# A hybrid decoder layer on one core: the bonus products of the recurrence move behind the projections that cover the inverse

## The chip, the core and the metric

The kernel runs on one core of a Trainium2 chip. The engines of that core are TensorE (PE, matmuls; PEld is its weight load), VectorE (DVE), ScalarE (ACT), GpSimd (POOL) and SyncE (SP, which here issues the DMAs). Every engine has its own queue and works it off in order; engines wait for each other through semaphores. The metric is the device time of one execution in microseconds; less is better.

## The reference

One layer for 512 prompt tokens and 8 x 8 sample tokens (576 columns in all), with 1024 channels. A normed input is projected by one large matrix `w_in`, whose columns feed three branches and their gates; the branches are merged and projected again. Only the first branch, an RWKV-7 recurrence with 16 heads of 64, is touched by the change:

```python
def step(s, inp):
    r_t, k_t, v_t, w_t, kk_t, a_t = inp
    sa = jnp.einsum("bhvk,bhk->bhv", s, -kk_t)
    s = (s * w_t[:, :, None, :] + sa[..., None] * (kk_t * a_t)[:, :, None, :]
         + v_t[..., None] * k_t[:, :, None, :])
    return s, jnp.einsum("bhvk,bhk->bhv", s, r_t)
...
bonus = jnp.sum(r * k * r_k.astype(f32), axis=-1, keepdims=True) * v
out = (o + bonus.reshape(bsz, t, RW_WIDTH)) * jax.nn.silu(z.astype(f32))
```

The `bonus` is a sum over the 64 channels of a head, times `v`. It is added to the recurrence's output only at the end; nothing in the recurrence needs it.

## The kernel before

**The stream of projections.** All projections by `w_in` are cut into units of 128 output channels (class `Unit`). The class `Stream` runs them in steps: one step is 6 matmuls of 128x288 (three products of high and low parts, two halves of the columns), and 8 steps make a unit. `st.go(n)` (L381) runs n steps, so PE has work while another engine prepares the next piece of the recurrence. There are two lists: units added with `st.add` go first, the others (gates `g`, `xb`, `zc`, `zb`) are fill, taken when the first list is empty. When a unit begins, the next one is picked and its weights are loaded (`weight`, L286): a DMA of 512 KB into `wraw`, a cast on ACT into `whi` (L293), and a subtraction on DVE into `wlo` (L294). `wraw`, `whi` and `wlo` have two buffers each, so the cast for a unit waits until PE has ended the unit before the one that begins.

**The recurrence.** `rwkv_phase` handles the 16 heads as 8 pairs, in four groups (0 to 3) of two pairs. The time axis is cut into chunks of 64. For each group, in the order of the code:
- `prep_a`, `prep_b`, `scaled`, `products`, `prep_c`: decay, keys and products of a chunk, the matrix `M1` among them.
- `substitute` (L1079): the inverse of the 32x32 triangular blocks, a chain of 30 pairs on DVE, a product into `Xt` (L1085) and an addition into `X` (L1087), each needing the one before. Then `X` is transposed into `XT` (L1091), and X and XT go by DMA to DRAM (`d2`, `d3`; both print as `d`) and back, into `M1` (L1101) and `xz` (L1098).
- `direct` (L1134): products R and Zt that need no inverse.
- `bonus` (L1011): for each pair of heads, `bonh` and `bonl` (high and low part of r k r_k), four matmuls with a block of ones into `bon`, and two products with `v` on DVE (L1020).
- `st.go(34)`: 34 steps of projections, the cover for the chain and its DMAs.
- `invert2` (L1104): products `z` and `w` of 32x32 that complete the inverse; `z` needs `xz`. It holds four steps of its own. `solved` (L1160): U and W.
- `lora_w(g + 1)` loads small weights of the next group, and `st.add(*group_units(g + 1))` puts its six projections (`u`, for k, r and v of two pairs) on the first list.
- `chain` (L1201), eight times: the chunks one after the other, with 2 and 4 steps of projections in each (1 and 3 in the last group). On DVE, `plus_state` (L1199) adds the state's part to UV, which the matmul `dS` then reads.
- Then `pairs(g + 1)` runs the stream until the next group's units are done, and `prep_a` of that group begins.

A framework orders the instructions of each engine by its own model of their times, unless `K.pin` is set: then PE keeps the order of the code. In the code before, it is set from `invert2` to the end of the chain. The output of a unit is taken by its `use`; that of a `u` unit needs copies on ACT and two operations on DVE (L923, L924).

Of the kernel before, what the change touches and what calls it, by code (L numbers as in the profile page):

```python
# [860 lines left out]
def rwkv_phase(K):  # L861
    nc, tc, i, pv, st = K.nc, K.tc, K.i, K.pv, K.st
    G = 2
    NG = KC // G
    H2 = 2 * NCH
    NQ = 2 * G * H2
    with ExitStack() as es:
# [65 lines left out]
        def group_units(g):  # L933
            out = []
            for tag, base in (("k", 8), ("r", 0), ("v", 16)):
                for p in range(G * g, G * g + G):
                    out.append(u_unit(base + p, tag))
            return out
# [46 lines left out]
        def prep_b(o):  # L985
            p, q = o.p, o.q
            br = o.br
            zs = 1 - q
            pr_ = K.psb("rs")
            for c in range(NCH):  # L990
                K.mm(pr_[br:br + 64, 2 * c:2 * c + 2], o.sq[:, C * c:C * c + C], K.bones2, start=True, stop=True,
                                 tile_position=(0, br))
            rvf = rsv[q][br:br + 64].rearrange("p c h -> p (c h)")
            nc.vector.tensor_scalar(rvf, pr_[br:br + 64, 0:18], -2.0, -2.0 * L2_EPS, op0=ALU.mult, op1=ALU.add)
            nc.vector.reciprocal(rvf, rvf)
            BK = o.BK = rg.tile([P, NCH, 2, C], F32, tag="BK", name="BK")
            ZR = o.ZR = rg.tile([P, NCH, 2, C], F32, tag="ZR", name="ZR")
            zn, ta, sq = o.zn, o.ta, o.sq
            nc.vector.tensor_mul(ZR[:, 0:8, zs, :], chk(zn)[:, 0:8, :], o.Pp[:, :, 0:C])
            nc.vector.tensor_mul(ZR[:, 8, zs, :].rearrange("p (b s) -> p b s", s=NS), smp(zn), o.Ps[:, :, 0:NS])  # L1000
            nc.vector.tensor_mul(ZR[:, 0:8, q, :], chk(o.r)[:, 0:8, :], o.Pp[:, :, 1:])
            nc.vector.tensor_mul(ZR[:, 8, q, :].rearrange("p (b s) -> p b s", s=NS), smp(o.r), o.Ps[:, :, 1:])
            nc.vector.scalar_tensor_tensor(sq, ta, 1.0, zn, op0=ALU.add, op1=ALU.mult)
            nc.vector.tensor_mul(BK[:, :, zs, :], chk(sq), chk(o.pinv))
            nc.scalar.activation(ta, ta, AF.Identity, scale=K.kah[:, p:p + 1], bias=K.kac[:, p:p + 1])
            nc.vector.tensor_mul(o.k, o.k, ta)
            nc.vector.tensor_mul(BK[:, :, q, :], chk(o.k), chk(o.pinv))
            nc.vector.tensor_mul(ta, o.r, o.k)
            o.bon = rg.tile([P, N], F32, tag="bon", name="bon")
# [12 lines left out]
        def scaled(o):  # L1022
            BK = o.BK
            BKn = o.BKn = rg.tile([P, NCH, P], F32, tag="BKn", name="BKn")
            for c in range(8):
                nc.scalar.activation(BKn[:, c, :], BK[:, c].rearrange("p w t -> p (w t)"), AF.Copy, scale=o.Pp[:, c, C:C + 1])
            nc.vector.tensor_mul(BKn[:, 8, :].rearrange("p (w b s) -> p w b s", w=2, s=NS),
                                 BK[:, 8].rearrange("p w (b s) -> p w b s", s=NS),
                                 o.Ps[:, :, NS:NS + 1].unsqueeze(1).to_broadcast([P, 2, NB, NS]))

        def products(o):

            q, BK, ZR = o.q, o.BK, o.ZR
            rv = rsv[q]
            M1 = o.M1 = rg.tile([P, H2, P], F32, tag="M1", name="M1")
            for c0, n in ((0, 4), (4, 4), (8, 1)):
                pms = [K.psb("m1") for h in range(2)]
                for c in range(c0, c0 + n):
                    for w in range(2):
                        for h in range(2):  # L1040
                            K.mm(pms[h][64 * w:64 * w + 64, P * (c - c0):P * (c - c0) + P],
                                             BK[64 * h:64 * h + 64, c, w, :],
                                             ZR[64 * h:64 * h + 64, c].rearrange("p a b -> p (a b)"), start=True, stop=True,
                                             tile_position=(64 * h, 64 * w))
                for h in range(2):
                    for c in range(c0, c0 + n):
                        nc.vector.scalar_tensor_tensor(M1[:, 2 * c + h, :], pms[h][:, P * (c - c0):P * (c - c0) + P],
                                                       rv[:, c, h:h + 1], maskq[q][c == 8],
                                                       op0=ALU.mult, op1=ALU.mult)
            for blk in range(2):  # L1050
                q0 = (blk * G + q) * H2
                a = o.br + 32 * blk
                nc.sync.dma_start(d1[0][q0:q0 + H2].rearrange("q s t -> s q t"), o.M1[a:a + 32, :, a:a + 32])
# [80 lines left out]
        def direct(prs):  # L1134

            r0 = prs[0].r0 = [rt.tile([P, N], F32, tag="k", name="r0") for _ in range(2)]
            for c0, n in ((0, 4), (4, 4), (8, 1)):
                pR = K.psb("R")
                for c in range(c0, c0 + n):
                    for h in range(2):  # L1140
                        for o in prs:
                            a, b, m = o.kr, o.br, P * (c - c0) + C * h
                            K.mm(pR[b:b + 64, m:m + C], o.M1[a:a + 64, 2 * c + h, b:b + 64],
                                             o.UV[a:a + 64, c, C * h:C * h + C], start=True, stop=True, tile_position=(a, b))
                if n == 4:
                    nc.scalar.copy(r0[c0 // 4][:, 0:P * n], pR)
                else:
                    for h in range(2):
                        nc.scalar.copy(r0[h][:, P * 4:N], pR[:, C * h:C * h + C])
            zt = prs[0].zt = [rt.tile([P, N], F32, tag="r", name="zt") for _ in range(2)]  # L1150
            for c0 in (1, 5):
                pZ = K.psb("Zt")
                for c in range(c0, c0 + 4):
                    for o in prs:
                        b, m = o.br, P * (c - c0)
                        K.mm(pZ[b:b + 64, m:m + P], o.ZR[:, c, 1 - o.q, :], K.ident, start=True, stop=True,
                                         tile_position=(0, b))
                nc.scalar.copy(zt[c0 // 4][:, 0:P * 4], pZ)
# [209 lines left out]
        for g in range(NG):  # L1368
            UV2[0] = rg.tile([P, G, NCH, P], F32, tag="UV", name="UV", bufs=1)
            d1[0] = dr.tile([NQ, 32, 32], F32, tag="d1", name="d1")  # L1370
            for o in prs:
                prep_b(o)
                st.go(3)
                scaled(o)
                products(o)
                st.go(3)
            X = invert()
            for o in prs:
                prep_c(o)
                st.go(3)  # L1380
            substitute(prs, X)
            direct(prs)
            for o in prs:
                bonus(o)
            st.go(34)
            K.pin = True
            invert2(prs)
            solved(prs)
            if g + 1 < NG:
                lora_w(g + 1)  # L1390
                st.add(*group_units(g + 1))
            o0, o1 = prs
            none = lambda: None
            fulls = {1: lambda: sample_a(o0), 4: lambda: sample_c(o0), 5: lambda: sample_a(o1)}
            tileds = {2: lambda: sample_b(o0), 3: lambda: [sample_o(o0), sample_in(o1)],
                      6: lambda: sample_b(o1), 7: lambda: sample_o(o1)}
            sample_in(o0)
            for c in range(8):
                chain(prs, c, (2, 4) if g + 1 < NG else (1, 3), fulls.get(c, none), tileds.get(c, none))
            K.pin = False  # L1400
            sample_c(o1)
            st.add(*[za_unit(o.p) for o in prs])
            nxt = pairs(g + 1) if g + 1 < NG else []
            for o in prs:
                state_out(o)
            gn_a()
            for o in nxt:
                prep_a(o)
                st.go(2)
            gn_t(prs)  # L1410
            for o in prs:
                gn_b(o)
            prs = nxt
# [70 lines left out]
def hybrid_step(ctx: ExitStack, tc: tile.TileContext, ins, outs):  # L1484
# [20 lines left out]
    with ExitStack() as es:  # L1505
# [34 lines left out]
        attention(K, pool(es, "xs"), qs, qf, kv)  # L1540
    K.softplus()
    rwkv_phase(K)
    st.until("zc7")
    o2 = pool(ctx, "o2")
# [66 lines left out]
```

## Time and profile before

| | us |
|---|---|
| median of 3 runs | 1204.92 |
| lowest and highest | 1202.93, 1207.01 |
| profiled execution | 1204.39 |
| its span | 1202.4 |
| PE busy | 1128.5 (94%) |
| DVE busy | 707.8 (59%) |
| ACT busy | 522.4 (43%) |

The mean granted clock of TensorE is 0.969 of full speed. A row of a timeline has the start, the duration, engine, line, operation, output<-input, shapes, count, and in brackets the idle time just before it with what ended it. A row of the waits has the total, the times and the longest. A row of the stretches has the length and then for PE, PEld, DVE, ACT and POOL the busy time and the count, then the granted clock, the busy share of the DMA engines and GB/s. All names of tiles are without buffer numbers.

### The profile page before, as it was taken

Reading aid. Unit: us, or ns where it says so; the run is one execution under the profiler, and the core shown is the slowest. Engines: PE = TensorE matmul, PEld = TensorE weight load, DVE = VectorE, ACT = ScalarE, POOL = GpSimd, SP = SyncE. Lnnn points to the kernel's source line nnn. Section 1 sums busy time; section 2 is a strip of 40 time slices with the busy share of each in tenths; the row PEclk is TensorE's granted clock in tenths of the full one; section 3 lists DMA queues with packets and bytes.
Section 4 is the critical chain, followed back from the end, with each engine's and each line's share of the span. In section 5 each row is a group of like instructions: output and inputs, shape, how many; then the busy total and the mean of one; then the engine's idle time right before and its main releaser. Section 6 shows DMA issues by size and latency. Waiting matters only on the chain.

```text
span 1202.4 us, 25686 instructions
## 1 busy us (share of the span) xinstructions
PE 1128.5 (94%) x10567; PEld 1066.5 (89%) x10567; DVE 707.8 (59%) x1454; ACT 522.4 (43%) x1004; POOL 152.7 (13%) x287
## 2 busy tenths in 40 slices
PE   5999999999979999969999789999799999999997
PEld 4998988899979998969998789989799999999997
DVE  5345655246773478734687724787456669684633
ACT  5444544246413374313464233653233576622333
POOL 3010000010001311002210003110032002020022
PEclk9999999999998998979999979999799999999999
DMA  4456756632242222332223423233434857466412
GB/s 138 127 193 194 227 176 226 201 94 80 76 142 75 68 65 88 107 94 82 67 81 93 131 64 89 64 88 100 128 105 139 284 151 219 130 218 188 123 46 79
DMA packets 220622, 151.49 MB, mean 126 GB/s; under 512 B 52640, under 2 KB 196106, under 8 KB 220506
## 3 DMA queue, kind: packets, MB, share of 16 engines
q1 hardware_dynamic: 217242, 146.87, 41.7%
q10 hardware_dynamic: 3264, 2.99, 0.9%
q8 instruction: 83, 1.36, 0.5%
q14 instruction: 33, 0.27, 0.1%
HBM read 120.82 MB, written 29.01 MB: 125 GB/s over the span
## 4 chain that ended last, share of the span: by engine, by line
PE 70%; DVE 14%; DMA 8%; ACT 4%; issue 3%; SPq 1%; ACTq 0%; DVEq 0%
PE u L71 14%; PE br L71 11%; PE g L71 7%; PE za L71 4%; PE fo L71 4%; PE q L71 4%; DVE wlo L294 3%; DVE X L1087 3%; DVE Xt L1085 3%; PE zc L71 2%; PE A L71 2%; PE zb L71 2%; PE xb L71 2%; PE kv L71 2%; DMA wraw<-in_w_mem_kv 1%
## 5 line engine op out<-in xcount | busy, mean ns | idle before, releaser
L293 ACT CAST whi<-wraw 128x1024 fp32r<-128x1024 f32 x129 | 135.2, 1048 | 284.8 <-issue 57.5
L294 DVE TENSOR_TENSOR wlo<-wraw,whi 128x1024 fp32r<-128x1024 f32 x128 | 156.7, 1224 | 168.3 <-ACT whi L293 167.0
L71 PE MATMUL u<-xh,whi 128*128 128x288 f32 x400 | 89.5, 305 | 0.0
L71 PE MATMUL g<-xh,whi 128*128 128x288 f32 x384 | 88.9, 312 | 0.0
L71 PE MATMUL g<-xh,wlo 128*128 128x288 f32 x384 | 87.4, 307 | 1.1 <-DVE wlo L294 1.1
L71 PE MATMUL g<-xl,whi 128*128 128x288 f32 x384 | 86.4, 306 | 0.0
L71 PE MATMUL u<-xl,whi 128*128 128x288 f32 x400 | 85.9, 296 | 0.0
L71 PE MATMUL u<-xh,wlo 128*128 128x288 f32 x400 | 85.8, 296 | 0.0
L71 PE MATMUL br<-oh,wlo 128*128 128x288 f32 x384 | 82.5, 297 | 1.4 <-DVE wlo L294 1.4
L71 PE MATMUL br<-oh,whi 128*128 128x288 f32 x384 | 83.5, 299 | 0.0
L71 PE MATMUL br<-ol,whi 128*128 128x288 f32 x384 | 82.2, 296 | 0.0
L71 PEld LDWEIGHTS u<-xh,whi 128*128 128x128 f32 x400 | 63.7, 189 | 6.5 <-issue 6.1
L71 PEld LDWEIGHTS g<-xh,wlo 128*128 128x128 f32 x384 | 64.8, 196 | 1.9 <-DVE wlo L294 1.3
L71 PEld LDWEIGHTS g<-xh,whi 128*128 128x128 f32 x384 | 64.7, 197 | 1.8 <-issue 1.0
L71 PEld LDWEIGHTS g<-xl,whi 128*128 128x128 f32 x384 | 64.6, 196 | 1.0 <-issue 1.0
L71 PEld LDWEIGHTS u<-xh,wlo 128*128 128x128 f32 x400 | 64.6, 188 | 0.0
L71 PEld LDWEIGHTS u<-xl,whi 128*128 128x128 f32 x400 | 64.5, 188 | 0.0
L71 PEld LDWEIGHTS br<-oh,wlo 128*128 128x128 f32 x384 | 61.8, 188 | 1.9 <-DVE wlo L294 1.9
L71 PEld LDWEIGHTS br<-oh,whi 128*128 128x128 f32 x384 | 62.2, 189 | 0.6
L71 PEld LDWEIGHTS br<-ol,whi 128*128 128x128 f32 x384 | 61.8, 188 | 0.0
L1199 DVE TENSOR_TENSOR UV<-A,UV 64x128 f32<-64x128 f32 x64 | 18.5, 289 | 56.6 <-PE A L71 55.5
L1265 POOL TENSOR_TENSOR zx<-ZR,bm 128x256 f32<-128x256 f32 x16 | 16.7, 1052 | 224.5 <-DVE X L1087 103.8
(390 smaller groups left out, 2888.6 us busy)
## 6 DMA issues: line engine op xcount, KB each, us to landing
wraw<-in_w_in SPq DMA_DIRECT2D x89, 512.0 KB
wraw<-in_w_mem_kv SPq DMA_DIRECT2D x16, 512.0 KB
kn<-in_cache_mem_k SPq DMA_DIRECT2D x16, 512.0 KB
kn<-in_cache_mem_v SPq DMA_DIRECT2D x16, 512.0 KB
gd<-flt SPq DMA_DIRECT2D x24, 288.0 KB
gtt<-gd SPq DMA_DIRECT2D x24, 288.0 KB
wraw<-in_w_br_c SPq DMA_DIRECT2D x8, 512.0 KB
wraw<-in_w_br_a SPq DMA_DIRECT2D x8, 512.0 KB
```

What stands on the lines that cost most here:

```text
L71: ins = self.nc.tensor.matmul(*a, **kw)
L293: nc.scalar.copy(hi, raw)
L294: eng.tensor_sub(lo, raw, hi.bitcast(F32))
L1085: nc.vector.tensor_mul(tv, X[:, 0:s, s:s + 1].to_broadcast([NQ, s, m]), X[:, s:s + 1, s + 1:].to_broadcast([NQ, s, m]))
L1087: nc.vector.tensor_add(X[:, 0:s, s + 1:], X[:, 0:s, s + 1:], tv)
L1199: nc.vector.tensor_add(u, pA[o.br:o.br + 64, P * o.q:P * o.q + P], u)
L1265: nc.gpsimd.tensor_mul(zx[:, w], o.ZR[:, 8, w, :].rearrange("p (g t) -> p g t", g=2).unsqueeze(2).to_broadcast([P, 2, 4, 32]), K.bm4.unsqu ...
```

## The change

The bonus products stand behind the cover instead of ahead of it, the cover is 36 steps instead of 34 and cut in two, and the next group's units are put on the first list after the first 26 of them, not behind `solved`. The pinned stretch now begins with the bonus.

```diff
             substitute(prs, X)
             direct(prs)
+            st.go(26)
+            if g + 1 < NG:
+                st.add(*group_units(g + 1))
+            st.go(10)
+            K.pin = True
             for o in prs:
                 bonus(o)
-            st.go(34)
-            K.pin = True
             invert2(prs)
             solved(prs)
             if g + 1 < NG:
                 lora_w(g + 1)
-                st.add(*group_units(g + 1))
```

How this moves the instructions is shown at group 1. PE before, from the end of `direct` (Zt) into the cover (`g`, a gate's unit):

```order
L71 MATMUL Zt<-ident,ZR 64x128 x16
L71 MATMUL bon<-bonh,bones 128x288
L71 MATMUL bon<-bonl,bones 128x288
L71 MATMUL bon<-bonh,bones 128x288
L71 MATMUL bon<-bonl,bones 128x288
L71 MATMUL bon<-bonh,bones 128x288
L71 MATMUL bon<-bonl,bones 128x288
L71 MATMUL bon<-bonh,bones 128x288
L71 MATMUL bon<-bonl,bones 128x288
L71 MATMUL g_5662<-xh,whi 128x288
```

PE now, at the end of the cover, from its last step (`g`) into `invert2` (`z`):

```order
L71 MATMUL g_6037<-xl,whi 128x288 x2
L71 MATMUL g_6037<-xh,wlo 128x288 x2
L71 MATMUL bon<-bonh,bones 128x288
L71 MATMUL bon<-bonl,bones 128x288
L71 MATMUL bon<-bonh,bones 128x288
L71 MATMUL bon<-bonl,bones 128x288
L71 MATMUL bon<-bonh,bones 128x288
L71 MATMUL bon<-bonl,bones 128x288
L71 MATMUL bon<-bonh,bones 128x288
L71 MATMUL bon<-bonl,bones 128x288
L71 MATMUL z_6104<-xz,M_5348 32x32
L71 MATMUL z_6105<-xz,M_5492 32x32
```

The eight matmuls of the bonus went from the head of the cover to its end, and the cover's first unit follows `direct` at once. DVE before, at the head of the chain (BKn is the last product of `prep_c`, `wls` belongs to `lora_w`):

```order
L1067 TENSOR_TENSOR BKn<-bkt,rsv_2642 128x128
L1020 TENSOR_TENSOR bon<-bon,v 128x288
L1085 TENSOR_TENSOR Xt<-X 72x30
L1088 MEMSET X 72x32
L1020 TENSOR_TENSOR bon<-bon,v 128x288
L1087 TENSOR_TENSOR X<-X,Xt 72x30
L1020 TENSOR_TENSOR bon<-bon,v 128x288
L1085 TENSOR_TENSOR Xt<-X 72x58
L1020 TENSOR_TENSOR bon<-bon,v 128x288
L1087 TENSOR_TENSOR X<-X,Xt 72x2x29
L628 TENSOR_TENSOR wls<-wl,wls 128x256
```

DVE now, at the eighth pair of the chain, where its first `wlo` stands, and at its end:

```order
L1085 TENSOR_TENSOR Xt<-X 72x184
L1087 TENSOR_TENSOR X<-X,Xt 72x8x23
L294 TENSOR_TENSOR wlo<-wraw,whi 128x1024
L1085 TENSOR_TENSOR Xt<-X 72x198
...
L1087 TENSOR_TENSOR X<-X,Xt 72x30
L1091 COPY XT<-X 36x1024
L294 TENSOR_TENSOR wlo<-wraw,whi 128x1024
L1020 TENSOR_TENSOR bon<-bon,v 128x288 x4
L628 TENSOR_TENSOR wls<-wl,wls 128x256
L294 TENSOR_TENSOR wlo<-wraw,whi 128x1024
```

The four products of the bonus and the `wls` left the chain and stand behind XT. The first `wlo` stood behind the seventh pair before, now behind the eighth; the fourth stood ahead of XT, now behind it. In group 0 the first `wlo` stands behind the fifth pair (the fourth before) and all four stay ahead of XT. On SP, in all four groups, X now goes to DRAM ahead of XT (before, in groups 0 and 3 alone), and in groups 1 to 3 the last weight load ahead of these DMAs is the one whose buffer the chain's third `wlo` frees (before, the fourth).

## The prediction

> **What bounds the kernel now.** I began with the page's busy times, then the waits of TensorE (PE), then the timelines around the longest of them.
>
> ```profile
> PE 1128.5 (94%) x10567; PEld 1066.5 (89%) x10567; DVE 707.8 (59%) x1454; ACT 522.4 (43%) x1004; POOL 152.7 (13%) x287
> ```
>
> PE is busy for 1128.5 of 1202.4 us, so only its waits and its speed can be won. Its list of waits (total, times, longest) starts so:
>
> ```profile
> PE z L71 <- DMA xz<-d: 37.4, 8, 8.7
> PE m L71 <- DVE M L1047: 5.7, 7, 1.2
> ```
>
> Half of PE's idle time is one wait: `z`, the first product of the inverse (`invert2`), waits for `xz`, twice in each of the four groups. PE's timeline at these places (start, duration, idle before):
>
> ```profile
> 360.66 0.31 PE L71 MATMUL z<-xz,M 32*32 32x32 f32 x2 [8.61 <-DMA xz<-d]
> 361.79 2.13 PE L71 MATMUL z<-xz,M 32*32 32x32 f32 x70 [0.82 <-DMA xz<-d]
> 527.94 0.31 PE L71 MATMUL z<-xz,M 32*32 32x32 f32 x2 [8.65 <-DMA xz<-d]
> 530.65 2.13 PE L71 MATMUL z<-xz,M 32*32 32x32 f32 x70 [2.40 <-DMA xz<-d]
> 692.86 0.31 PE L71 MATMUL z<-xz,M 32*32 32x32 f32 x2 [8.10 <-DMA xz<-d]
> 694.91 2.12 PE L71 MATMUL z<-xz,M 32*32 32x32 f32 x70 [1.74 <-DMA xz<-d]
> 855.35 0.31 PE L71 MATMUL z<-xz,M 32*32 32x32 f32 x2 [6.47 <-DMA xz<-d]
> 856.25 2.12 PE L71 MATMUL z<-xz,M 32*32 32x32 f32 x70 [0.60 <-DMA xz<-d]
> ```
>
> The waits are 9.43, 11.05, 9.84 and 7.07 us by group. The cover ran out at 352.05 in group 0 (360.66 - 8.61), and at 519.29, 684.76 and 848.88. Each wait costs more than itself. Busy times by stretch, with the granted clock as the figure after POOL's, from each fall of the clock to its return:
>
> ```profile
> 355.80:372.20 16.40, 10.72 (x168) 9.97 (x168) 0.00 (x0) 3.43 (x9) 0.54 (x1) 0.50 0.32 66
> 523.40:539.70 16.30, 9.36 (x163) 8.82 (x164) 0.00 (x0) 3.12 (x8) 0.00 (x0) 0.50 0.37 78
> 690.10:703.70 13.60, 9.10 (x162) 8.56 (x163) 0.00 (x0) 3.12 (x8) 0.00 (x0) 0.50 0.32 62
> 854.00:867.40 13.40, 11.46 (x180) 10.64 (x182) 0.00 (x0) 4.17 (x10) 0.00 (x0) 0.50 0.47 110
> ```
>
> The clock falls to 0.50 some 3.8 to 5.3 us after the cover's end and stays there for 13 to 16 us. What that does to projections is seen in these rows, six matmuls (one step) apart in each pair of rows:
>
> ```profile
> 349.49 0.43 PE L71 MATMUL g<-xh,whi 128*128 128x288 f32 x2
> 350.29 0.43 PE L71 MATMUL g<-xh,whi 128*128 128x288 f32 x2
> ...
> 369.25 0.68 PE L71 MATMUL g<-xh,whi 128*128 128x288 f32 x2
> 370.69 0.68 PE L71 MATMUL g<-xh,whi 128*128 128x288 f32 x2
> ```
>
> A step takes 0.80 us at the full clock and 1.44 at half. `invert2` holds four steps, so a fallen clock costs 4 x 0.64 = 2.6 us in a group, beside the wait.
>
> **What holds `xz`.** The DVE chain of `substitute` (30 pairs of L1085 and L1087), then the copy XT, then the DMAs to `d` and back. DVE and ACT, groups 0 and 1:
>
> ```profile
> 322.53 0.18 DVE L1085 TENSOR_TENSOR Xt<-X 72x30 f32<-72x30 f32 x1
> ...
> 327.03 0.46 DVE L1020 TENSOR_TENSOR bon<-bon,v 128x288 f32<-128x288 f32 x1 [4.26 <-PE bon L71]
> ...
> 330.55 1.23 DVE L294 TENSOR_TENSOR wlo<-wraw,whi 128x1024 fp32r<-128x1024 f32 x1 [0.36 <-ACT whi L293]
> 331.69 0.28 DVE L1085 TENSOR_TENSOR Xt<-X 72x130 f32<-72x130 f32 x1
> ...
> 332.33 0.31 DVE L1085 TENSOR_TENSOR Xt<-X 72x150 f32<-72x150 f32 x1
> ...
> 354.72 1.03 DVE L1091 COPY XT<-X 36x1024 f32<-36x1024 f32 x1
> ...
> 492.26 0.46 DVE L1020 TENSOR_TENSOR bon<-bon,v 128x288 f32<-128x288 f32 x1 [3.70 <-PE bon L71]
> ...
> 501.30 0.36 DVE L1085 TENSOR_TENSOR Xt<-X 72x198 f32<-72x198 f32 x1
> ...
> 521.13 1.02 DVE L1091 COPY XT<-X 36x1024 f32<-36x1024 f32 x1
> ```
> ```profile
> 329.46 1.05 ACT L293 CAST whi<-wraw 128x1024 fp32r<-128x1024 f32 x1 [1.76 <-PE g L71]
> 496.70 1.05 ACT L293 CAST whi<-wraw 128x1024 fp32r<-128x1024 f32 x1 [3.77 <-PE g L71]
> ```
>
> Two things stand in the chain's way: the bonus product `bon`, for which DVE idles 4.26 and 3.70 us, and `wlo` (L294), which stands in the middle of the chain and waits for ACT's cast `whi`, which waits for PE to end a unit (the buffers of `whi` are two).
>
> **Part 1: `bon` leaves the head of the chain.** By the order, DVE's four products now stand behind XT, after the chain. The chain can begin at 322.5 and 488.6 (492.26 - 3.70) with no stop for `bon`. But it does not gain the whole 4 us. In group 0 `wlo` now stands behind pair 5, in groups 1 to 3 behind pair 8. Before, four pairs with four `bon` and a `wls` between them took from 327.03 to 330.55, 3.5 us, and pair 5 took 0.64. So in group 0 the chain reaches `wlo` by 326.7 at the latest, and in group 1 (three pairs more, under 0.9 each: their operations are no longer than the 0.36 of pair 9) by 495.4. `whi` comes later than either: it waits for the end of the unit under way, and that moves up only by the eight `bon` matmuls that no longer stand ahead of it on PE:
>
> ```profile
> 326.46 0.40 PE L71 MATMUL bon<-bonh,bones 128*128 128x288 f32 x1
> ...
> 327.63 0.43 PE L71 MATMUL g<-xh,wlo 128*128 128x288 f32 x2
> ```
>
> That is 1.17 us. So `whi` starts at 328.29, `wlo` 1.09 later (330.55 - 329.46), the next pair 1.14 after that (331.69 - 330.55): pair 6 at 330.5, where it stood at 332.33: 1.8 us won. In group 1: 496.70 - 1.17 + 1.09 + 1.14 = 497.8 for pair 9 instead of 501.30: 3.5 won. Groups 2 and 3 by the same sum, from these rows:
>
> ```profile
> 662.17 1.05 ACT L293 CAST whi<-wraw 128x1024 fp32r<-128x1024 f32 x1 [3.77 <-PE xb L71]
> 826.29 1.05 ACT L293 CAST whi<-wraw 128x1024 fp32r<-128x1024 f32 x1 [4.31 <-PE g L71]
> ```
> ```profile
> 666.01 0.36 DVE L1085 TENSOR_TENSOR Xt<-X 72x198 f32<-72x198 f32 x1
> ...
> 685.83 1.02 DVE L1091 COPY XT<-X 36x1024 f32<-36x1024 f32 x1
> ...
> 828.90 0.36 DVE L1085 TENSOR_TENSOR Xt<-X 72x198 f32<-72x198 f32 x1
> ...
> 848.74 1.55 DVE L1091 COPY XT<-X 36x1024 f32<-36x1024 f32 x1
> ```
>
> 663.2 instead of 666.01 (2.8) and 827.4 instead of 828.90 (1.6). In groups 1 to 3 the fourth `wlo` moreover stands behind XT instead of before it: 1.14 each. XT so ends earlier by 1.8, 4.7, 3.9 and 2.7 us, 13.1 together. The later `wlo` (a unit of eight steps, 6.4 us, apart on PE) come before the chain reaches them by the same sum; were they late, 1.17 a group and the 1.14 would be left, 8.1.
>
> The products themselves cost nothing on DVE behind XT: DVE has no other work while PE waits for `xz`. On PE the eight matmuls only change sides of the cover.
>
> **Part 2: 36 steps for 34.** Work is moved, not added: 2 x 0.80 = 1.6 us a group run while PE waited, 6.4 us in all. They are missing later in stretches where PE waits for nothing.
>
> **Part 3: the transfers behind XT.** From XT's end to the second `z`: 6.04 us in group 0 (355.75 to 361.79), 8.50 in group 1, 8.06 in group 2, 5.96 in group 3 (850.29 to 856.25). In groups 1 and 2 SP issued 512 KB of weights just before, and `d` from XT ahead of `d` from X:
>
> ```profile
> 520.52 0.38 SPq L61 DMA_DIRECT2D wraw<-in_w_in  x1
> 522.18 0.32 SPq L1094 DMA_DIRECT2D d<-XT  x1
> ```
>
> In the changed order the last weight load ahead of these DMAs in groups 1 to 3 is the one that waits for the third `wlo`, not the fourth, and X goes first in all four: I take 6.0 everywhere, 4.6 us won (bounds 0 and 5.5). In group 0 a weight load now waits for a later `wlo` and lies closer to them: 0.5 lost (bounds 0 and 2.5, the excess of group 1 over 6.0).
>
> **Part 4: the next group's projections 14 steps earlier.** They take the place of other units, step for step; the last of them now ends with the chain of chunks, not behind it, and the same number of steps covers what follows. Their buffers `k` and `r` come free with U and W, before the first unit ends. I count nothing; the rivals bound it.
>
> Sum: 13.1 + 6.4 + 4.6 - 0.5 = 23.6 us. By group: 2.9, 8.8, 7.6 and 4.3, so that 6.5, 2.2, 2.2 and 2.8 us of waiting stay, 13.8 in all.
>
> **Part 5: the clock.** In group 0 a gap of 6.5 us is past the 3.8 to 5.3 at which the clock fell. In groups 1 to 3 a gap of 2.2 to 2.8 is under it. But `z` and `w` (32x32) seem hardly to count as work: PE was busy for 9 to 11 us inside each of the slow stretches. Gap and the 2.1 us of `z` make 4.3 to 4.9, within 3.8 to 5.3. I take two of the three groups as spared: 5.2 us. Bounds 0 and 10.4, no group or all four.
>
> The profiled execution took 1204.39 us (1202.4 of span, 2.0 around it), the median is 1204.92. 1204.4 - 23.6 - 5.2 = 1175.6; on the median's scale **1176**.
>
> **The rivals.**
> *A, the forecast* (0.41): 1170 to 1184, by how many groups lose the clock and by part 3.
> *F, a gap shorter than the fall's delay keeps the clock in all of groups 1 to 3*, whatever `z` counts for: 1204.4 - 23.6 - 7.8 = 1173.0. For it: gaps of 2.2 to 2.8 against delays of 3.8 to 5.3. Against: the slow stretches went on for 13 to 16 us while PE worked, so small products may count as a gap. 0.25.
> The Trainium skill (TensorE: Matmul & The Clock Gate, "What's actually happening") has the clock fall after a whole idle window of about 3.4 us and return after one busy window, which would be F; the fall agrees with the rows here (3.8 to 5.3 us), the return after one window does not (13 to 16 us).
> *B, the chain is not held by `wlo`* and the whole wait goes: 1204.4 - 37.4 - 10.4 = 1156.6. For it: 4 us of DVE idle and 1.8 of `bon` are removed from each chain. Against: `wlo` still stands inside it. 0.08.
> *C, each `wlo` holds the chain and the transfers stay as slow*: 8.1 + 6.4 = 14.5, and the clock falls everywhere: 1190. 0.15.
> *D, PE waits for DVE in the chain of chunks instead.* All six units of the next group now end within it, and by the order their L923 and L924 stand ahead of the addition L1199, for which PE's `dS` waits; whoever is late there stops PE in a pinned order. The nearest price is PE's wait for M, up to 1.2 us (the row above): seven chunks by four groups by 1.2 is 33.6, and the time 1176 + 33.6 = 1209.6, slower. It decides from 28.8 / 28 = 1.03 us a chunk. Against: two steps lie between, and no such wait is in the list now, with five units there. 0.06.
> *E, no change*: what D costs eats the gain, 1201 to 1208. 0.05.
>
> **How the numbers follow.** A measurement of this kernel can tell about 0.3%, 3.6 us, from no change. A, F, B and C are faster: 0.89; E 0.05; D 0.06. The range goes from 1166 (F with the clock kept in group 0 too and the bounds of part 3) to 1192 (all of C); B, D and E are left out, 0.19.
>
> **What would show it.** Right: DVE idle ahead of the chain's first `wlo`, 2 to 4 us, released by ACT `whi`; no idle for `bon`; XT 2 to 5 us earlier in its group; PE's wait for `xz` near 14 us, most of it in group 0; granted clock at 1.00 behind most inverses. Wrong: the wait for `xz` at 0 (B), above 20 (C), or new waits of PE for L1199 (D).

## The result and the profile after

The changed kernel takes 1197.58 us (median of 6 runs, 1192.96 to 1197.97) against 1205.13 for the kernel before (6 runs beside it, 1202.93 to 1207.01): 0.9929 of its time, 95% interval 0.9908 to 0.995. It is 7.5 us faster, where 29 were forecast. The profiled execution took 1197.7 us with a span of 1196.0, which is 6.4 less than before.

The waits of TensorE (total, times, longest) in the changed kernel:

```profile
PE z L71 <- DMA xz<-d: 17.7, 8, 6.2
PE pg L71 <- issue: 6.4, 1, 6.4
...
PE m L71 <- DVE M L1047: 5.7, 7, 1.2
...
PE dS L71 <- DVE UV L1199: 3.5, 3, 1.3
...
PE ot L65 <- ACT flt L416: 2.3, 2, 1.2
PE ot L65 <- DVE onat L1318: 1.5, 2, 1.1
```

The wait that the change is about fell from 37.4 to 17.7 us, a gain of 19.7. Beside it stand waits that the kernel before did not have, or hardly: ahead of `pg` 6.4 (0.3 before), ahead of `dS` 3.5 (none), ahead of `ot` 3.8 (1.3). Here `pg` is the first product of the phase behind the recurrence, `dS` the update of the state in a chunk, and `ot` the transposes of a group's output. What is left of the wait at `z` by group, the rows of `z` in PE's timeline:

```profile
361.22 0.28 PE L71 MATMUL z<-xz,M 32*32 32x32 f32 x2 [6.24 <-DMA xz<-d]
362.17 2.09 PE L71 MATMUL z<-xz,M 32*32 32x32 f32 x70 [0.67 <-DMA xz<-d]
519.55 0.21 PE L71 MATMUL z<-xz,M 32*32 32x32 f32 x2 [2.16 <-DMA xz<-d]
521.00 1.95 PE L71 MATMUL z<-xz,M 32*32 32x32 f32 x70 [1.24 <-DMA xz<-d]
682.51 0.22 PE L71 MATMUL z<-xz,M 32*32 32x32 f32 x2 [2.73 <-DMA xz<-d]
683.79 1.29 PE L71 MATMUL z<-xz,M 32*32 32x32 f32 x70 [1.06 <-DMA xz<-d]
841.02 0.22 PE L71 MATMUL z<-xz,M 32*32 32x32 f32 x2 [2.80 <-DMA xz<-d]
842.01 2.04 PE L71 MATMUL z<-xz,M 32*32 32x32 f32 x70 [0.77 <-DMA xz<-d]
```

That is 6.91, 3.40, 3.79 and 3.57 us. The stretches with the clock at half are shorter, but all four that stand behind `z` are still there. Their busy times (PE, PEld, DVE, ACT, POOL) and, behind them, the granted clock:

```profile
357.40:371.00 13.60, 9.11 (x162) 8.63 (x163) 0.57 (x1) 4.77 (x11) 0.00 (x0) 0.50 0.35 68
521.20:531.40 10.20, 10.20 (x167) 9.52 (x163) 1.56 (x2) 5.01 (x11) 0.00 (x0) 0.50 0.26 68
685.00:691.80 6.80, 6.80 (x95) 6.44 (x91) 0.56 (x1) 4.31 (x11) 0.00 (x0) 0.51 0.24 53
842.00:852.40 10.40, 10.39 (x167) 9.72 (x168) 1.89 (x2) 4.72 (x10) 0.00 (x0) 0.51 0.50 137
```

The new wait at `pg` stands at the start of the phase behind the recurrence. Rows of its timeline, all engines in order of time:

```profile
930.07 0.36 ACTq L505 DMA_DIRECT2D xe<-xbd  x1
...
936.08 0.67 ACT L627 CAST oh<-oxl 128x576 fp32r<-128x576 f32 x1 [5.34 <-DMA oxl<-ocz]
...
937.20 2.54 ACT L627 CAST oh<-oxl 128x576 fp32r<-128x576 f32 x4
...
939.65 0.88 ACT L511 ACTIVATE cva<-xe,par 128x600 f32<-128x600 f32 x1
...
944.18 0.75 DVE L515 SCALAR_TENSOR_TENSOR xc<-xe,par,cva 128x512 f32<-128x512 f32 x1
...
945.02 0.82 PE L71 MATMUL pg<-xc,wbd 128*128 128x288 f32 x1 [6.41 <-issue]
```

ACT waits 5.34 us for a load of `oxl` (the output of the third branch, read back from DRAM). `xe`, the input of the first convolution, is loaded from ACT's own queue at 930.07 and has landed when POOL reads it at 933.22. But the convolution's first operation, L511, stands in ACT's queue behind seven casts of `oxl` (L627), and so behind that wait. The convolution ends with `xc` (L515, L517), and `pg` needs `xc`. PE ran out of projections at 938.61 (945.02 - 6.41).

The new waits at `dS` are in the last group alone. ACT and DVE, then PE, at the first of them:

```profile
864.47 0.65 ACT L423 ACTIVATE flt<-zc 128x576 f32<-128x576 f32 x1
864.47 1.23 DVE L294 TENSOR_TENSOR wlo<-wraw,whi 128x1024 fp32r<-128x1024 f32 x1 [1.07 <-ACT whi L293]
865.73 0.75 DVE L424 SCALAR_TENSOR_TENSOR flt<-flt,zc 128x576 f32<-128x576 f32 x1
866.51 0.61 DVE L1199 TENSOR_TENSOR UV<-A,UV 64x128 f32<-64x128 f32 x2
```
```profile
864.21 0.61 PE L71 MATMUL A<-sbd,ZR 128*128 128x128 f32 x4
...
866.96 0.56 PE L71 MATMUL dS<-UV,BKn 128*64 128x64 f32 x8 [1.34 <-DVE UV L1199]
```

`A`, the chunk's product with the state, had ended at 864.82, so L1199 could have run. But a projection (`zc`) had ended in the step just ahead of `A` (ACT reads its result from 864.47), and on DVE the low part of the next weights (L294) and L424, which takes the projection's result, stand ahead of L1199. One step of projections between `A` and `dS` does not cover them.

The difference between the two profiled executions, term by term: xz -19.7; the stretch from the second `z` to `U` -1.1 (40.6 to 39.4, the four groups together; from the start of the last row of `z`); the waits of `W`, gone, -1.3; `pg` +6.1 and the stretch behind it +1.5 (from the first `pg` to the first `fo`, the output projection, 187.2 us in place of 185.7, half clock again); `dS` +3.5; `ot` +2.5; the start up to the first `R`, which the change does not touch, +1.3. The sum is -7.2, the spans differ by -6.4; the 0.8 us between them stay open.

### The profile page after: what moved, and what is told of

Read it like the earlier page. It is cut to its first block, busy times and chain, and to the rows that moved or that the text cites. A ratio compares the mean times of both kernels' runs of the same rounds, so it can differ in the third digit from the quotient of the medians.

```text
span 1196.0 us, 25701 instructions
## 1 busy us (share of the span) xinstructions
PE 1129.9 (94%) x10567; PEld 1066.6 (89%) x10567; DVE 707.7 (59%) x1454; ACT 522.0 (44%) x1004; POOL 163.7 (14%) x287
## 4 chain that ended last, share of the span: by engine, by line
PE 69%; DVE 13%; DMA 8%; ACT 5%; issue 5%; SPq 1%; POOL 0%; ACTq 0%; DVEq 0%
PE u L71 13%; PE br L71 11%; PE g L71 6%; PE za L71 4%; PE fo L71 4%; PE q L71 4%; PE kv L71 2%; PE zc L71 2%; PE A L71 2%; PE zb L71 2%; DVE X L1087 2%; DVE wlo L294 2%; DVE Xt L1085 2%; PE xb L71 2%; PE pg L71 1%
## 5 line engine op out<-in xcount | busy, mean ns | idle before, releaser
L294 DVE TENSOR_TENSOR wlo<-wraw,whi 128x1024 fp32r<-128x1024 f32 x128 | 159.2, 1244 | 177.2 <-ACT whi L293 166.3
L1265 POOL TENSOR_TENSOR zx<-ZR,bm 128x256 f32<-128x256 f32 x16 | 20.4, 1287 | 256.6 <-DVE X L1087 136.5
L1199 DVE TENSOR_TENSOR UV<-A,UV 64x128 f32<-64x128 f32 x64 | 18.5, 288 | 48.3 <-PE A L71 47.1
```

Source lines behind the costliest of these rows:

```text
L294: eng.tensor_sub(lo, raw, hi.bitcast(F32))
L1199: nc.vector.tensor_add(u, pA[o.br:o.br + 64, P * o.q:P * o.q + P], u)
L1265: nc.gpsimd.tensor_mul(zx[:, w], o.ZR[:, 8, w, :].rearrange("p (g t) -> p g t", g=2).unsqueeze(2).to_broadcast([P, 2, 4, 32]), K.bm4.unsqu ...
```

## The experiments

My theory was at first: the parts of the prediction add up, and the end of the recurrence gives some of the gain back. The rivals are told with each run. Ratios are to the kernel before, with 95% intervals. A profiled execution can be several us from its median: the start up to the first `R`, the same in all of them, took 319.9 to 327.4 us.

**The bonus products moved, nothing else.** The products stand behind 34 steps, the queueing stays behind `solved`:

```
+            st.go(34)
+            K.pin = True
             for o in prs:
                 bonus(o)
-            st.go(34)
-            K.pin = True
```

> The kernel before with one part of the change: the bonus products stand behind the 34 projection steps; the next group's projections are queued where they were, behind solved. Theory S (the prediction's parts add up, and the end of the recurrence gives some of it back): the move alone is worth the 13.1 us of part 1 in the wait ahead of xz (37.4 to about 24), the order of units at the end of the recurrence is that of before, so the wait ahead of pg stays near 0.3 us and the time is about 1205 - 13 = 1192 us, faster than the whole change. Rival W (the chain stays with each wlo in any case): the wait ahead of xz falls by under 5 us, about 1201 us.

Measured: 1188.28 us, 0.9873 (0.9854 to 0.9891), faster than the whole change. The xz wait is 23.4 us, that ahead of `pg` 0.3. The move by itself takes 14.0 us off the wait and 15.3 us off the time (by the ratio), where part 1 forecast 13.1; rival W falls.

**The early queueing alone.**

```
             st.go(26)
+            if g + 1 < NG:
+                st.add(*group_units(g + 1))
             st.go(8)
```

> The kernel before with one part of the change: the next group's projections are queued behind 26 of the 34 steps; the bonus products stay ahead of the steps. Theory S, with the prediction's part 4 taken as right: nothing changes that ends last, the wait ahead of xz stays near 37 us and the time within 2 us of 1205. Rival Q (queueing earlier shifts where the units' ends fall against the chain of chunks and brings the new waits ahead of dS and ot): slower by 3 to 6 us, 1208 to 1211, with waits of 2 to 5 us ahead of dS and ot that before does not have. Either way the wait ahead of pg stays under 1 us if it belongs to the two extra steps.

Measured: 1206.77 us, 1.002 (1.0008 to 1.0031). The xz wait is 39.0; waits ahead of `ot` come to 4.5 us (1.3 before), and none ahead of `dS`. So the queueing brings the waits at `ot`, and a small loss by itself, but it is not the source of those at `dS`.

**36 steps and the move, without the early queueing.**

```
-            st.go(26)
-            if g + 1 < NG:
-                st.add(*group_units(g + 1))
-            st.go(10)
+            st.go(36)
...
                 lora_w(g + 1)
+                st.add(*group_units(g + 1))
```

> The whole change without its early queueing: 36 steps, then the bonus products; the next group's projections are added behind solved, as before. Theory S: the early queueing counts for nothing, the wait ahead of xz is near 18 us, that ahead of pg near 6, and the time 1196 to 1199. Rival Q: the waits ahead of dS (3.5) and ot (2.5) go, and the time is 1190 to 1193.

Measured: 1203.52 us, 1.0002 (0.9986 to 1.0019): neither, and no faster than before. Two steps more than the move alone, and 15 us slower. Its waits at `pg` (13.1 us together) and `dS` (3.5) account for that:

```profile
PE z L71 <- DMA xz<-d: 24.4, 8, 8.8
PE pg L71 <- issue: 10.6, 1, 10.6
...
PE dS L71 <- DVE UV L1199: 3.5, 3, 1.3
PE pg L71 <- DVE xc L515: 2.5, 1, 2.5
```

Here the count of units in program order tells why. Between two `R` the kernel before runs 125.5, 128 and 128 steps. A unit of 8 steps, once begun or picked to come next, is run before the next group's projections get their turn, and `st.until` runs the stream until the last of these is done; with 36 steps and the late queueing one more unit of the filling list is begun, so each of the first three groups runs 8 steps more (133.5, 136 and 136). Early queueing takes that back: the changed kernel runs 125.5, 128 and 128. In the last group, with nothing left to queue, the two steps begin one more unit all the same: 100.8 steps up to the last `ro` instead of 92.8 (`ro` are the transposes that end the recurrence). What is used up there stood between `ro` and `pg`: 22 steps before, 14 in the changed kernel, 8 in this one, where 18 more are taken from behind `pg`. The time from `ro` to `pg` hardly follows: 19.6 us before, 18.0 in the changed kernel, 17.4 here. It is the chain of the loads of `oxl`, ACT's casts and the first convolution, and the steps are its cover. This is theory U of the runs that follow: projections are moved in whole units, and those that run earlier are missing at `pg`.

**The first convolution ahead of the loads of `oxl`.** The changed kernel, with this in the phase behind the recurrence:

```
         K.pin = True
         conv(0)
+        load_c()
```

where `load_c` is the load and split (cast and low part) of `oxl` that stood ahead of the phase.

> The changed kernel with one edit behind the recurrence: the first convolution (its load of xe and the operations on it) stands ahead of the eight loads and splits of oxl, not behind them. Theory S (the pg wait of 6.4 us is gain given back, since the load of xe stands behind ACT's wait for oxl): the wait ahead of pg falls under 1 us, nothing takes its place, and the time is about 1191.5 us. Rival L (the loads behind the recurrence are bound by the transfers, so that a wait moves on to the first br or a later pg): the sum of PE's waits between the last ro and the first br stays near 6 us and the time within 2 us of 1197.6.

Measured: 1193.6 us, 0.9911 (0.9894 to 0.9928). The wait ahead of `pg` is 3.1 us, half of what it was, and no new wait of PE takes its place, but from `pg` to `fo` it takes 188.7 us in place of 187.2. The gain is 4.0 us by the medians and 2.2 by the ratios, where 6 were expected. The reason given in the expectation was not right: in the changed kernel the load of `xe` was issued ahead of ACT's long wait already. What moved is L511, which now stands behind four casts of `oxl` instead of seven; the third of these still waits 4.70 us for its load, so PE still reaches `pg` before the first convolution is through.

**34 steps in the last group alone.**

```
-            st.go(10)
+            st.go(10 if g + 1 < NG else 8)
```

> The changed kernel with 34 steps in the last group alone (36 in the three others). Theory U (the two extra steps are lost in the last group: a whole projection is used up there that stood ahead of pg, and its evacuation falls on the chain of chunks): 22 steps stand between ro and pg again, the wait ahead of pg falls from 6.4 to under 1 us, the waits ahead of dS (3.5) go, the last xz wait grows by 1.6 us; 6.4 + 3.5 - 1.6 = 8.3 us, about 1189 us. Rival L (the loads behind the recurrence and the chunks hold the end, whatever stands ahead of them): pg waits for as long as before, 1196 to 1199.

Measured: 1188.53 us, 0.9864 (0.9841 to 0.9887). The wait ahead of `pg` is 0.3, the waits ahead of `dS` are gone, xz is at 19.3. So two steps in the last group cost the changed kernel 9 us by the medians; the changes in the three waits (6.1 + 3.5 - 1.6) make 8.0. Theory U holds.

**34 steps in every group, with the move and the early queueing** (`st.go(8)` in place of `st.go(10)`).

> The changed kernel with 34 steps in every group: the moved bonus products and the early queueing without the two extra steps. Theory U: the early queueing alone costs the waits ahead of ot (about 2.5 to 4 us more than with the move alone), the xz waits are those of the move alone (near 23 us), no wait ahead of pg; about 1188.3 + 3 = 1191 us, and 36 steps in three groups are worth 1.5 to 4 us more than this. Rival N (the queueing costs nothing behind the moved products): 1188.

Measured: 1191.59 us, 0.9885 (0.9865 to 0.9905). The xz wait is 23.6, `ot` 4.4 (1.3 with the move alone). Beside the run before it, two steps in the first three groups are worth 3.1 us by the medians; beside the first run, the queueing costs 3.3. The single runs overlap in both cases (1186.08 to 1192.35 and 1186.53 to 1194.45, against 1190.11 to 1192.49 here), so that the waits, 4.3 us at `z` and 3.1 at `ot`, are the better evidence.

**42 steps in the first three groups, 34 in the last.**

```
-            st.go(10)
+            st.go(16 if g + 1 < NG else 8)
```

> The changed kernel with 42 steps in the first three groups and 34 in the last: the waits ahead of xz in groups 1 and 2 should be gone (below 0.7 us). The clock: theory I (it falls because of the 32x32 products and the waits behind them, whatever the wait at z) expects the granted clock still at half for 5 to 8 us behind these inverses; rival F (it falls because PE waits at z) expects full clock behind the inverses of groups 1 and 2. The time: theory U expects one to two projections fewer ahead of pg (14 steps, 6 us of wait there), so the gain at z (3.4 + 3.8 + part of 6.9 us) is mostly given back: 1186 to 1192 us. Rival L, where cover is not given back: under 1184.

Measured: 1187.29 us, 0.9846 (0.982 to 0.9872). There is no wait at `z` in groups 1 and 2, and no half clock behind them: theory I falls, F holds. `pg` waits 8.5 us (14 steps ahead of it). One thing was not expected: in the last group the wait at `z` is 10.9 us, as in the run with 36 steps without early queueing (9.4), though there were 34 steps. In both, `zc` projections alone stand under that cover; in the other runs so far it begins with 20.8 steps of `g`.

**42 steps in the last group, 36 in the others** (`st.go(10 if g + 1 < NG else 16)`).

> The changed kernel with 42 steps in the last group (36 in the others): a whole projection more than 34. The units then end at the same places in the chain of chunks as with 34, and 14 steps stand ahead of pg as in the changed kernel. Theory U, with the dS waits owed to where the projections end: dS waits gone (3.5), the last xz wait gone (3.6), pg still waiting 6 us; about 1190.5 us. Rival P (the dS waits come from the later units' weights or from the pace of the chain, not from the place of the ends): dS still waits 3 to 4 us, about 1194.

Measured: 1189.05 us, 0.986 (0.9836 to 0.9885). No wait ahead of `dS`, none at the last `z`, 6.5 ahead of `pg`. Eight steps more than 34 leave the chunks as they were, two do not: the waits at `dS` come from where the projections end.

**The same, with the first convolution ahead of the loads.**

> The changed kernel with 42 steps in the last group, as in the run before, and with the first convolution ahead of the eight loads and splits of oxl. Theory U: the two edits touch different waits and add up: no wait ahead of the last xz, none ahead of dS, pg waiting 3 us in place of 6.5; 1189 - 3.4 = about 1185.6 us. Rival L (behind the recurrence the loads are the bound): the wait goes on elsewhere and the time stays at 1189.

Measured: 1183.02 us, 0.9818 (0.979 to 0.9847); `pg` waits 4.2 us, and PE's other waits are nearly those of the run before. The two edits add up within the noise: 8.5 and 4.0 us singly, 14.6 together.

**`zc` projections under the last group's cover.** The move alone, with the list that fills in another order:

```
-    return zb + g[:16] + xb + g[16:-4] + zc + g[-4:]
+    return zb + g[:16] + xb + zc + g[16:]
```

> The move of the bonus products alone (34 steps, queued as before) with the eight zc projections ahead of g10 to g17 in the list that fills, so that zc1 to zc5 stand under the last group's cover, where g11 to g13, zc0 and zc1 stood. Theory Z (each zc unit that ends there adds its two DVE operations, 1.3 us, to the elimination's chain): the last xz wait grows from 5.2 to 9 or 10 us, half clock behind it for 17 us in place of 10. Rival: it stays near 5 us, and the 9 to 11 us of the runs with fewer projections left have another cause. Besides, 14 steps in place of 22 stand ahead of pg, so theory U expects a wait of about 6 us there; together about 1199 us, and 1194 by the rival.

Measured: 1201.38 us, 0.9973 (0.9957 to 0.999). The last group's wait at `z`, and the first of four such pairs on DVE in the middle of the chain of `substitute`:

```profile
846.31 0.28 PE L71 MATMUL z<-xz,M 32*32 32x32 f32 x2 [10.00 <-DMA xz<-d]
847.53 2.09 PE L71 MATMUL z<-xz,M 32*32 32x32 f32 x70 [0.93 <-DMA xz<-d]
```
```profile
815.17 0.74 DVE L424 SCALAR_TENSOR_TENSOR flt<-flt,zc 128x576 f32<-128x576 f32 x1
...
816.11 0.75 DVE L428 SCALAR_TENSOR_TENSOR flt<-flt 128x576 f32<-128x576 f32 x1
```

10.9 us in place of 5.2, and 6.5 at `pg`: theory Z holds. The kind of work under a cover matters, not only its length: the result of a `g` projection is taken out (evacuated) by ACT, that of a `zc` one by ACT and two DVE operations in the chain that it covers. From `R` to XT's end the chain takes 36.8 us, 30.3 with the move alone. The four pairs are 6.0 us of DVE work; but two more `wlo` (2.4 us) and the four bonus products (1.8) also come to stand ahead of XT, and the run does not separate the shares.

**42 steps with one step fewer in each chunk.** The groups use up as many units as before, since the chunks of the first three groups run five steps, not six:

```
-chain(prs, c, (2, 4) if g + 1 < NG else (1, 3), fulls.get(c, none), tileds.get(c, none))
+chain(prs, c, (2, 3) if g + 1 < NG else (1, 3), fulls.get(c, none), tileds.get(c, none))
```

First with 34 steps in the last group and the loads as they are:

> 42 steps in the first three groups with 2 and 3 steps in each chunk, 34 steps in the last group, the loads behind the recurrence left as they are: the number of projections used up in each group is that of the kernel before, 22 steps stand ahead of pg. Theory U: xz waits 1.8 us in group 0, none in groups 1 and 2, 5 us in the last; no wait ahead of pg or dS; 19.3 - 6.8 = 12.5 us less than with 36, 36, 36 and 34 steps, about 1176 us. Rival C (chunks short of steps): 1180 to 1185.

Measured: 1170.28 us, 0.9709 (0.9682 to 0.9736), better than expected by 6 us. Then with 42 steps in every group and the first convolution ahead of the loads:

> 42 steps in every group, one step fewer in each chunk of the first three groups (2 and 3 in place of 2 and 4, so that each group uses up as many projections as in the changed kernel), and the first convolution ahead of the loads of oxl. Theory U: the xz wait is left in group 0 alone (1.8 us), pg waits 3 us, the chain of chunks goes without the eight steps; 17.7 - 1.8 + 3.5 + 3.3 = 22.7 us less than the changed kernel, 1175 us. The clock: theory F (half clock follows the wait at z) expects full clock behind the inverses of groups 1 to 3. Rival C (the chain of chunks is short of steps and waits for DVE ahead of W, dS or A): 3 to 8 us of new waits there, 1178 to 1183.

Measured: **1164.05 us, 0.9657 (0.9631 to 0.9683)**: 40 us faster than the kernel before and 33 faster than the changed kernel. Its waits where the changed kernel had its largest, and where rival C of these two runs expected new ones:

```profile
PE A L71 <- DVE sbd L1227: 2.8, 4, 0.8
PE pg L71 <- POOL conv_st L507: 2.4, 1, 2.4
PE A L71 <- DVE UV L1175: 2.0, 3, 0.7
...
PE z L71 <- DVE wls L629: 1.2, 1, 1.2
...
PE z L71 <- DMA xz<-d: 0.7, 1, 0.7
```

The chunks do wait 4.8 us ahead of `A`, as this C has it, but the sums of both left out the clock. PE behind `z` in group 1, the changed kernel and then the run with 42 steps and 34 in the last group:

```profile
521.00 1.95 PE L71 MATMUL z<-xz,M 32*32 32x32 f32 x70 [1.24 <-DMA xz<-d]
...
524.62 2.13 PE L71 MATMUL w<-M,xz 32*32 32x32 f32 x72
...
531.30 2.20 PE L71 MATMUL U<-r,M 64*64 64x64 f32 x66
```
```profile
515.09 1.67 PE L71 MATMUL z<-xz,M 32*32 32x32 f32 x72
...
517.68 1.33 PE L71 MATMUL w<-M,xz 32*32 32x32 f32 x72
...
521.53 2.14 PE L71 MATMUL U<-r,M 64*64 64x64 f32 x66
```

From these rows of `z` to `U` it is 10.3 us there and 6.4 here, for the same work (but for two products of `z`). The four groups together: 39.4 in the changed kernel, 32.2 here, 28.3 with 42 steps everywhere. The last is 11.1 us less, as much as the 11 by which 1164 lies below the 1175 expected. That the two agree so well is partly luck, since smaller terms cancel: `ot` won 3.5 us that no sum had, and the chunks lost 4.8. The stretches of the run with 34 steps in the last group, behind `z` in groups 1 to 3, with the granted clock, 1.00 where nothing waited and half where the last group still did:

```profile
515.00:525.20 10.20, 10.08 (x308) 9.23 (x306) 3.24 (x8) 6.27 (x16) 0.62 (x4) 1.00 0.26 64
667.60:677.80 10.20, 10.08 (x307) 9.27 (x308) 3.24 (x8) 6.26 (x16) 0.83 (x6) 1.00 0.25 63
820.00:830.00 10.00, 10.00 (x156) 9.32 (x153) 0.00 (x0) 3.69 (x9) 0.00 (x0) 0.51 0.44 117
```

## Why the prediction was wrong

**Part 1, `bon` leaves the chain's head: right.** From the first `R` to XT's end it took 33.4, 34.6, 33.8 and 33.2 us before and 31.4, 30.3, 30.3 and 30.3 after: 2.0, 4.3, 3.6 and 2.9 won, 12.8 together, where 13.1 were forecast. What held the chain is what the prediction said; DVE in groups 0 and 1 of the changed kernel:

```profile
330.83 1.23 DVE L294 TENSOR_TENSOR wlo<-wraw,whi 128x1024 fp32r<-128x1024 f32 x1 [4.21 <-ACT whi L293]
...
493.23 1.23 DVE L294 TENSOR_TENSOR wlo<-wraw,whi 128x1024 fp32r<-128x1024 f32 x1 [2.56 <-ACT whi L293]
```

DVE idles 4.21 and 2.56 us for `whi`. The run with this part alone gave it by itself.

**Part 3, the transfers: mis-sized.** From XT's end to the second `z` I took 6.0 us, and 0.5 more in group 0; it was 7.1, 6.7, 7.1 and 6.8. So the transfers won 0.8 us together, where 4.1 were forecast (4.6 - 0.5). That is 3.2 us of the 3.9 between the 13.8 us forecast for the xz wait and the 17.7 measured. Why they stayed above 6.0 with X first in all groups is open.

**Part 2, 36 steps: the step that failed.** The 1.6 us a group at `z` were won (23.4 to 17.7 against the move alone, 5.7 in place of 6.4). But "they are missing later in stretches where PE waits for nothing" was wrong, because steps don't come singly. Two steps in the last group begin a whole further projection, 8 steps, ahead of `ro`; at `pg`, where the 22 steps of before just covered the loads' chain (0.3 us of wait), 14 are left. I had looked for what is late next in the recurrence, and not at the first stretch behind it. Together with the waits at `dS`, which come from the same two steps, the last group's part of the change cost 9 us (1197.58 against 1188.53). Of the 22.4 us by which the spans' difference (6.4) falls short of the 28.8 forecast, this step has 11.1 (6.1 and 1.5 at and behind `pg`, 3.5 at `dS`); the clock has 4.1, the wait at `z` 3.9 and `ot` 2.5.

**Part 4, the next group's projections earlier: "I count nothing" was wrong in both directions.** By itself the queueing costs 1.6 us, and some 3 beside the moved products, through the waits at `ot`. Beside 36 steps it is worth 5.9 us (1203.52 against 1197.58), since it keeps the two steps from beginning one more unit in each of the first three groups too.

**Part 5, the clock: wrong.** I took two groups as spared, 5.2 us; none was, and the stretches to `U` became 1.1 us shorter together. The waits left in groups 1 to 3 were 3.4 to 3.8 us and not 2.2 to 2.8, but that is not the reason: with 42 steps the wait left in group 0 was 1.8 to 2.2 us, and the clock fell behind it all the same. So the mark of 3.8 to 5.3 us that I read from the time between the cover's end and the fall was no mark; only a group without a wait was spared. That the small products hardly count as work was nearer to what the runs show (last section). The price was too low as well: a group without a wait runs from `z` to `U` in 6.4 to 6.7 us, one with a wait in 8.9 to 10.5, so the clock costs 2.5 to 4.1 us, where I had put 2.6.

Rival D named the right place, L1199 ahead of `dS`, but a wrong reach: three waits of up to 1.34 us in the last group, where there is one step between, and none in the three groups it spoke of; what stands ahead of L1199 there is L294 and L424, not L923 and L924. Rival E had a time near the measured one (1201) and a true half, that new waits eat gain; C's mechanism (each `wlo` late) did not take place, but its two other conditions nearly did: the transfers won only 0.8 us, and the clock fell everywhere. Rival F fell with the clock.

## What to carry to other kernels

When work is drawn from a queue to cover a wait, count in the queue's own units what runs up to each later wait, and look at the first wait behind the loop: what covers here is missing there, and a wait that shows 0.3 us may have no slack at all. Ask too where the units end and which engine evacuates them, since that engine's queue may carry the very chain that is being covered. And when a part of a wait is removed that also slows the clock, it pays to remove the rest: the last 16 us of waiting at `z` brought another 11 with them.

## What the runs showed of the hardware that was not expected

The clock fell behind every wait at `z`, however short, and the small products alone did not bring it down. With the same 72 `z` and 72 `w` products of 32x32, it stayed at full in the nine groups without a wait (groups 1 and 2 in the three runs with 42 steps there, the last group in the three with 42 in that one), whose stretches from `z` to `U` took 6.4 to 6.7 us, and fell to half behind every group with one. The shortest waits among these were 0.74 and 1.04 us (42 and 34 steps, group 0) and 1.23 and 0.73 (42 steps everywhere, group 0), and behind the latter:

```profile
362.60:369.60 7.00, 7.00 (x94) 6.66 (x93) 0.00 (x0) 2.13 (x6) 0.00 (x0) 0.51 0.48 124
```

Two us of waiting around `z` were enough for 7 us at half clock, though PE was busy in all of them. But a short wait alone is no sure cause. Between changes of the clock lie multiples of 3.41 us, and counted in such windows the changed kernel kept the full clock over one with 1.88 us of wait and 128x288 products besides (from 678.2), while the run with 42 and 34 steps and five-step chunks lost it after one with 0.89 us of wait and 1.60 us of `z` (from 358.8). Of three waits of 1.16 us ahead of `m`, a product of `products` (at 461.1, 620.5 and 781.9 in the changed kernel), only the second was followed by half clock, 6.8 us from 623.63. So waits and small products seem to count together; what a window must hold for the clock to fall stays open.

The lengths behind `z` come in steps: 6.8, 10.2, 13.7 and 17.1 us, once 20.5. The Trainium skill (TensorE: Matmul & The Clock Gate, "What's actually happening") has a free-running window of about 3.4 us that decides; steps of 3.4 agree with it. That one busy window brings the clock back does not agree if all busy time counts: in the second stretch of the changed kernel PE was busy for all of 10.2 us. It does agree if the products of 32x32 do not count. Behind `z`, in all the traces, the last window of a stretch holds at most 1.07 us of `z` and `w`, and each window before it holds a wait or at least 1.44 us of them.
